# Four instead of three seven-product pairs in four of eleven gate and up groups of a two-layer decoder trunk

## The chip, the cores and the metric

The kernel runs on one core of a Trainium2 chip. The metric is the device time of one execution in microseconds (us). A core has a matrix engine (TensorE, PE in the profile), a vector engine (VectorE, DVE), a scalar engine (ScalarE, ACT), a general one (GpSimd, POOL) and a queue engine that issues most transfers (SP). Matmuls write into a separate memory (PSUM), which this kernel divides into two pools (`pa`, `pm`) of four tiles of 128 x 512 floats, called banks here; everything else lies in the core's main on-chip memory.

## The reference

Two decoder layers over 256 positions with 2048 features, in fp32. Each layer is a mixer (layer 0: sliding-window attention beside an mLSTM memory; layer 1: forgetting attention) and a SwiGLU feed-forward part (FFN), each behind an RMS norm and added to the residual stream h. The change touches the FFN:

```
def swiglu(xn, w_gate, w_up, w_down):
    return (jax.nn.silu(xn @ w_gate) * (xn @ w_up)) @ w_down
...
        h = h + swiglu(rms_norm(h, norm_ffn[layer]), w_gate[layer], w_up[layer], w_down[layer])
```

The hidden width is 5632, which is 11 blocks of 512.

## The kernel before

**Precision by three matmuls.** Each fp32 operand is split into a rounded high part (a cast on ScalarE, `hi`, `xh`, `mh`, `ht`) and a rest (a subtraction on VectorE, `lo`, `xl`, `ml`, `lt`). A product is then high by high, high by low and low by high: three matmuls into one bank (`three`). Weights come from memory as raw tiles of two k blocks (2 x 128 rows by 512 columns) and are split on the way.

**Seven products instead of eight.** `pair_group` computes two outputs at once, for example a gate block and an up block of 512 columns, each for two halves of the positions (t = 0, 1). For a *pair* of k blocks that is a 2 x 2 by 2 x 2 block product: eight block products, 24 matmuls. A *mixed* pair takes seven, 21 matmuls, after a scheme of the Strassen kind (Winograd's form): four sums of the weight blocks are formed on VectorE for each mixed pair (lines 568 to 571; `t`, `raw`) and split into `ht` and `lt`; four sums of the activations are formed once per layer by `sums_of` and kept in `sx`. Four of the seven products go into four banks of their own (`prods`), three straight into the result's banks (`plain`); at the group's end `combine` (lines 523 to 530) adds the `prods` into a tile `c` in four ways, then `c` and `plain` are added. A group therefore holds all eight banks: four from the pool `pa`, four from `pm`, changing roles from group to group.

**Order.** `ORDER` lists for a group of eight pairs which are mixed (1) and which plain (0): pairs 1, 3 and 5 are mixed, at the second, fourth and sixth place. The 11 gate and up groups of a layer (0 to 10) are taken in parts, `PARTS = (0, 3, 7, 11)`; after each part follow the two halves of the down product over the part's rows, also in `pair_group`, with two mixed pairs of six in the first part and three of eight in the others. The silu of the gate times the up result (`c`) is turned by DMA transposes of 16-bit planes, joined by copies on ScalarE (lines 646 and 653), split into `mh` and `ml`, and read by the down product; the last group of the first part is turned on TensorE. In the last down half of layer 0, `split_scaled` transposes h on TensorE for the next layer.

The order of the instructions on each engine isn't written out: a scheduler in the framework places every instruction by its own estimate of when its inputs are ready, and each engine then follows that order. The buffers that limit how far the splits run ahead are six `hi` and six `lo` tiles, two `ht`, two `lt`, and four raw tiles for mixed pairs.

Names and lines that the prediction uses: `hi` cast L177 and `lo` L178 (`split_chunk`), the same for other tiles L339 and L340 (`split_plain`), the weight sums L568 to L571, the combine L525 to L529, sums of `c` and `plain` L619, silu L621 and product L623, byte-plane copies L646 and L653, h and c L708, h and `plain` L353, transposes of h L275, the three matmuls of a product L509 to L511.

Of the kernel before, what the change touches and what calls it, by code (L numbers as in the profile page):

```python
# [17 lines left out]
P = 128  # L18
# [17 lines left out]
ORDER = ((0, 0), (1, 1), (0, 2), (1, 3), (0, 4), (1, 5), (0, 6), (0, 7))  # L36
DOWN = {
# [35 lines left out]
def trunk(  # L73
# [179 lines left out]
    def sums_of(pool, sh, sl, copies, full=None, tags=("tmp", "tmp"), bufs=None, box=None):  # L253
# [12 lines left out]
        split_plain(sh, sl, s)  # L266

    def split_scaled(idx, n, extra=None, joined=None):
        for half in range(2):
# [13 lines left out]
            if extra is not None and pair in mixed_of(ORDER):  # L283
                sh, sl, pool = extra
                j = mixed_of(ORDER).index(pair)

                def copies(full):
                    for i in range(2):
                        g = gT[:, idx * KT + 2 * pair + i : idx * KT + 2 * pair + i + 1]
                        nc.scalar.mul(full[:, i, :], pt[:, i, :, :].rearrange("p t q -> p (t q)"), g)  # L290

                sums_of(pool, sh[:, j, :, :], sl[:, j, :, :], copies)
# [200 lines left out]
    def out_proj(w, idx, key, extra):  # L493
        last, rest = KT - 4, []
        for n0 in (0, 2):
# [3 lines left out]
            for i in range(2):  # L499
# [3 lines left out]
                    (LATER[n0 + i], split_turned(idx, n0 + i, *scrap(extra[2], n0 + i), extra))  # L503
                )
                square_sum(key, n0 + i)
        return rest

# [8 lines left out]
    def pair_group(fp, par, lhs, sums, mats, order, todo=(), halves=None, inner=None, raws=None):  # L516
        plain = [[bank(par, "acc") for _ in range(NT)] for _ in range(2)]
        todo = list(todo)
# [4 lines left out]
        def combine(prods):  # L523
            c = fp.tile([P, 4, NB], F32, tag="c", name="c", bufs=1)
            nc.scalar.copy(c[:, 0, :], prods[0])  # L525
            nc.vector.tensor_tensor(out=c[:, 2, :], in0=prods[3], in1=c[:, 0, :], op=ALU.add)
# [5 lines left out]
        for pos, (kind, pair) in enumerate(order):  # L532
# [4 lines left out]
            if not kind:  # L537
# [4 lines left out]
                for m, (w, c0) in enumerate(mats):  # L542
                    hi, lo = load_chunk(w, k0, c0, NB)
                    run_due(todo, pos)
                    for i, t in walk:
# [4 lines left out]
                            pos == 0 and i == 0, last and i == CK - 1,  # L550
# [38 lines left out]
            three(plain[0][0], xb[:, t0], lb[:, t0], hg[:, 1, :], lg[:, 1, :], False, False)  # L589
            three(plain[1][0], sh[:, 3, :], sl[:, 3, :], hu[:, 1, :], lu[:, 1, :], False, False)  # L590
            three(prods[1], sh[:, 0, :], sl[:, 0, :], ht[0], lt[0], first, last)
            three(prods[2], sh[:, 2, :], sl[:, 2, :], ht[1], lt[1], first, last)
            three(prods[3], sh[:, 1, :], sl[:, 1, :], ht[2], lt[2], first, last)
            three(plain[0][1], xb[:, t1], lb[:, t1], ht[3], lt[3], False, False)
# [4 lines left out]
    def ffn(layer, fp, sx, sd, key, todo, idx_next=None, key_next=None, finish=None):  # L599
        r = rstd(key)  # L600

        def sums_x(pair):
            j = mixed_of(ORDER).index(pair)
            return sx[0][:, j, :, :], sx[1][:, j, :, :]

        for g0, g1 in zip(PARTS, PARTS[1:]):
# [3 lines left out]
            for g in range(g0, g1):  # L610
                par = (g1 - 1 - g) % 2
                plain, c = pair_group(
                    fp, par, x_of, sums_x, [(w_gate[layer], g * NB), (w_up[layer], g * NB)], ORDER, todo
                )
                todo = []
                for m in range(2):
                    for t in range(NT):
                        o = c[:, 2 * m + t, :]
                        nc.vector.tensor_tensor(out=o, in0=plain[m][t], in1=o, op=ALU.add)  # L619
                for t in range(NT):  # L620
                    nc.scalar.activation(c[:, t, :], c[:, t, :], AF.Silu, scale=r[:, t : t + 1])  # L621
                for t in range(NT):
                    nc.vector.scalar_tensor_tensor(  # L623
                        out=c[:, t, :], in0=c[:, 2 + t, :], scalar=r[:, t : t + 1], in1=c[:, t, :], op0=ALU.mult, op1=ALU.mult
# [47 lines left out]
            def sums_d(pair, order=order):  # L672
                j = mixed_of(order).index(pair)
                return sd[0][:, j, :, :], sd[1][:, j, :, :]
# [16 lines left out]
            for n0 in (0, 2):  # L691
# [20 lines left out]
    def close_layer(layer, w_out, idx, key, **rest):  # L712
        with tc.tile_pool(name=f"fp{layer}", bufs=2) as fp:
# [3 lines left out]
            todo = out_proj(w_out, idx, key, (*sx, fp))  # L717
            sd = [fp.tile([P, nd, 4, P], F32R, tag=f"sd{i}", name=f"sd{i}", bufs=1) for i in range(2)]
            ffn(layer, fp, sx, sd, key, todo, **rest)
# [22 lines left out]
    with tc.tile_pool(name="ev", bufs=1) as ev:  # L742
# [223 lines left out]
        with tc.tile_pool(name="mp", bufs=1) as mp:  # L966
            def sums_m(pair):
                j = mixed_of(MIXQ).index(pair)
                return sx[0][:, j, :, :], sx[1][:, j, :, :]
# [129 lines left out]
    with tc.tile_pool(name="od", bufs=1) as od:  # L1099
# [65 lines left out]
        def sums_x(pair):  # L1165
            j = mixed_of(MIX).index(pair)
            return sx[0][:, j, :, :], sx[1][:, j, :, :]
# [154 lines left out]
```

## Time and profile before

| | |
|---|---|
| median of 3 runs | 2077.48 us (2077.07 to 2077.85) |
| span of the profiled execution, first to last instruction | 2076.6 us |
| its own time | not given apart from the span |
| mean granted TensorE clock | 0.999 of full speed |
| memory traffic | 198 GB/s over the span |

The page lists busy time by engine, a row of tenths for 40 slices of the span, the chain of work that ended last, and the costliest groups of instructions with the idle time ahead of them and what ended it. Views of the trace cut the same records by window, line or tile; a timeline row gives the start in us, the duration, the engine, the line, output and input, and in brackets the idle time before it and who ended that. Matmuls overlap in the pipeline: a row of 0.39 us can start 0.23 us after the one before, so the distance of starts counts. A row of VectorE or ScalarE may overlap the next by some 0.08 us in the same way. Waits are put down to the last releaser.

### The profile page before, as it was taken

Reading aid. Unit: us, or ns where it says so; the run is one execution under the profiler, and the core shown is the slowest. Engines: PE = TensorE matmul, PEld = TensorE weight load, DVE = VectorE, ACT = ScalarE, POOL = GpSimd, SP = SyncE. Lnnn points to the kernel's source line nnn. Section 1 sums busy time; section 2 is a strip of 40 time slices with the busy share of each in tenths; the row PEclk is TensorE's granted clock in tenths of the full one; section 3 lists DMA queues with packets and bytes.
Section 4 is the critical chain, followed back from the end, with each engine's and each line's share of the span. In section 5 each row is a group of like instructions: output and inputs, shape, how many; then the busy total and the mean of one; then the engine's idle time right before and its main releaser. Section 6 shows DMA issues by size and latency. Waiting matters only on the chain.

```text
span 2076.6 us, 26994 instructions
## 1 busy us (share of the span) xinstructions
PE 2066.4 (100%) x9473; PEld 1715.0 (83%) x9473; DVE 1824.5 (88%) x2410; ACT 1374.7 (66%) x1736; POOL 41.7 (2%) x66
## 2 busy tenths in 40 slices
PE   9999999999999999999999999999999999999998
PEld 7878888888888888888888888888888888888887
DVE  6788769999999999999899778689999999999994
ACT  6777678765676656667676776687655667456763
POOL 1010000000000000000000001000000000000000
PEclk9999999999999999999999999999999999999999
DMA  8566577666566666666576866586665667666764
GB/s 292 172 213 188 190 247 236 203 217 206 189 230 223 205 210 205 220 212 204 185 215 204 235 193 184 156 283 220 206 205 200 213 206 234 203 202 213 220 197 138
DMA packets 309575, 434.87 MB, mean 209 GB/s; under 512 B 106412, under 2 KB 114624, under 8 KB 309312
## 3 DMA queue, kind: packets, MB, share of 16 engines
q1 hardware_dynamic: 307088, 426.27, 65.1%
q0 software_dynamic: 1632, 5.80, 0.8%
q8 instruction: 74, 1.21, 0.2%
q10 hardware_dynamic: 720, 1.09, 0.2%
q14 instruction: 61, 0.50, 0.1%
HBM read 408.68 MB, written 2.12 MB: 198 GB/s over the span
## 4 chain that ended last, share of the span: by engine, by line
PE 97%; DVE 1%; ACT 1%; DMA 1%; issue 1%; SPq 0%; POOLq 0%; POOL 0%; ACTq 0%; DVEq 0%
PE acc L510 21%; PE acc L509 21%; PE acc L511 21%; PE acc L213 5%; PE acc L212 5%; PE acc L214 5%; PE prod L509 5%; PE prod L510 5%; PE prod L511 5%; PE p L369 1%; PE po L470 1%; DMA raw<-in_w_in_odd_dram 0%; ACT s L403 0%; PE po L471 0%; DVE lo L178 0%
## 5 line engine op out<-in xcount | busy, mean ns | idle before, releaser
L177 ACT CAST hi<-raw 128x1024 fp32r<-128x1024 f32 (+3 forms) x656 | 664.8, 1028 | 440.2 <-PE acc L511 269.1
L178 DVE TENSOR_TENSOR lo<-raw,hi 128x1024 fp32r<-128x1024 f32 (+3 forms) x656 | 772.8, 1192 | 146.3 <-ACT hi L177 143.5
L510 PE MATMUL acc<-lo,xh 128*128 128x512 f32 x1254 | 488.6, 390 | 0.0
L509 PE MATMUL acc<-hi,xh 128*128 128x512 f32 x1254 | 485.9, 390 | 0.5 <-ACT hi L177 0.5
L511 PE MATMUL acc<-hi,xl 128*128 128x512 f32 x1254 | 484.8, 389 | 0.0
L510 PEld LDWEIGHTS acc<-lo,xh 128*128 128x128 f32 x1254 | 235.4, 188 | 49.4 <-DVE lo L178 0.6
L509 PEld LDWEIGHTS acc<-hi,xh 128*128 128x128 f32 x1254 | 235.2, 188 | 49.5 <-ACT hi L177 0.7
L511 PEld LDWEIGHTS acc<-hi,xl 128*128 128x128 f32 x1254 | 235.4, 188 | 48.8
L510 PE MATMUL acc<-lo,mh 128*128 128x512 f32 x437 | 169.7, 389 | 0.0
L511 PE MATMUL acc<-hi,ml 128*128 128x512 f32 x437 | 168.4, 389 | 0.0
L509 PE MATMUL acc<-hi,mh 128*128 128x512 f32 x437 | 167.9, 389 | 0.0
L339 ACT CAST hi<-raw 128x512 fp32r<-128x512 f32 x109 | 67.6, 620 | 89.4 <-PE acc L511 80.5
L213 PE MATMUL acc<-lo,mh 128*128 128x512 f32 (+1 forms) x322 | 126.3, 392 | 0.0
L212 PE MATMUL acc<-hi,mh 128*128 128x512 f32 (+1 forms) x322 | 125.8, 391 | 0.0
L214 PE MATMUL acc<-hi,ml 128*128 128x512 f32 (+1 forms) x322 | 123.7, 391 | 0.0
L340 DVE TENSOR_TENSOR lt<-t,ht 128x1024 fp32r<-128x1024 f32 x95 | 115.8, 1219 | 5.2 <-ACT ht L339 5.1
L339 ACT CAST ht<-t 128x1024 fp32r<-128x1024 f32 x95 | 99.9, 1051 | 30.7 <-PE prod L511 28.8
L339 ACT CAST ht<-raw 128x1024 fp32r<-128x1024 f32 x95 | 99.7, 1050 | 29.7 <-PE acc L511 15.0
L340 DVE TENSOR_TENSOR lt<-raw,ht 128x1024 fp32r<-128x1024 f32 x95 | 115.7, 1218 | 1.8 <-ACT ht L339 1.8
L213 PE MATMUL acc<-lo,xh 128*128 128x512 f32 (+3 forms) x288 | 99.8, 348 | 0.2 <-DVE lo L178 0.2
L214 PE MATMUL acc<-hi,xl 128*128 128x512 f32 (+3 forms) x288 | 98.1, 344 | 0.0
L212 PE MATMUL acc<-hi,xh 128*128 128x512 f32 (+3 forms) x288 | 95.9, 347 | 0.3
(363 smaller groups left out, 3448.0 us busy)
## 6 DMA issues: line engine op xcount, KB each, us to landing
raw<-in_w_gate_dram SPq DMA_DIRECT2D x176, 512.0 KB, 4.5
raw<-in_w_up_dram SPq DMA_DIRECT2D x176, 512.0 KB, 4.6
raw<-in_w_down_dram SPq DMA_DIRECT2D x176, 512.0 KB, 5.1
raw<-in_w_in_odd_dram SPq DMA_DIRECT2D x88, 512.0 KB, 4.9
raw<-in_w_in_even_dram SPq DMA_DIRECT2D x51, 512.0 KB, 5.0
raw<-in_w_out_even_dram SPq DMA_DIRECT2D x32, 512.0 KB, 5.1
raw<-in_w_out_odd_dram SPq DMA_DIRECT2D x32, 512.0 KB, 4.8
hr<-in_w_in_even_dram SPq DMA_DIRECT2D x12, 512.0 KB, 4.6
```

The source lines that it names most:

```text
L177: latest[0] = nc.scalar.copy(hi[:, k, 0:n], raw[:, k, 0:n])
L178: nc.vector.tensor_tensor(out=lo[:, k, 0:n], in0=raw[:, k, 0:n], in1=hi[:, k, 0:n].bitcast(F32), op=ALU.subtract)
L212: nc.tensor.matmul(o, ah[:, ts], hi, start=(k == 0), stop=False)
L213: nc.tensor.matmul(o, ah[:, ts], lo, start=False, stop=False)
L214: nc.tensor.matmul(o, al[:, ts], hi, start=False, stop=(k == k_all - 1 and cs.stop == n))
L339: nc.scalar.copy(dst_h, src)
L340: nc.vector.tensor_tensor(out=dst_l, in0=src, in1=dst_h.bitcast(F32), op=ALU.subtract)
L369: nc.tensor.matmul(pq[j % 2][:, j // 2, :], q_of(j, b), k_of(j)[:, 0:cols], start=True, stop=True)
L470: nc.tensor.matmul(po, v_of(j, 0), tt[:, j, 0:2, :].rearrange("p c q -> p (c q)"), start=True, stop=False)
L509: nc.tensor.matmul(o, ah, hi, start=start, stop=False)
L510: nc.tensor.matmul(o, ah, lo, start=False, stop=False)
L511: nc.tensor.matmul(o, al, hi, start=False, stop=stop)
```

## The change

In groups 1, 4, 6 and 8 of each layer (`DENSE`) a fourth pair, number 7, is mixed as well. The order of these groups (`HEAVY`) begins with a mixed pair and alternates. The activation sums of pair 7 are made when the others are (in `split_scaled`); three of the four sums are stored in those blocks of `xh` and `xl` that no product of the FFN reads, the t = 1 halves of the first k block of the mixed pairs 1, 3 and 5 (`rooms`), the fourth in a small tile `x4`. To make room for it the descriptor space of POOL's transfers is halved. Whether a matmul is the first into a bank (`start`) is now found by a record (`fresh`).

Where `halves` isn't used, that is in all FFN groups, `combine` has another layout of `c` (t before m) and other association: two sums of 512 columns and one of 1024 in place of four of 512. The sums of h and `c` in the down halves become two of 1024 instead of four of 512. `four` hands the sums over as lists; `sums_d` and the mixers' `sums_m` and `sums_x` use it with no change of meaning.

```
+HEAVY = ((1, 1), (0, 0), (1, 3), (0, 2), (1, 5), (0, 4), (1, 7), (0, 6))
+FOURTH = 7
+DENSE = (1, 4, 6, 8)
...
-    def sums_of(pool, sh, sl, copies, full=None, tags=("tmp", "tmp"), bufs=None, box=None):
+    def sums_of(pool, sh, sl, copies, full=None, tags=("tmp", "tmp"), bufs=None, box=None, x4=None):
...
-        split_plain(sh, sl, s)
+        if x4 is None:
+            split_plain(sh, sl, s)
+        else:
+            split_plain(sh, sl, s[:, 0:3, :])
+            split_plain(x4[:, 0, :], x4[:, 1, :], s[:, 3, :])
...
-            if extra is not None and pair in mixed_of(ORDER):
-                sh, sl, pool = extra
-                j = mixed_of(ORDER).index(pair)
+            if extra is not None and (pair in mixed_of(ORDER) or pair == FOURTH):
+                sh, sl, x4, pool = extra
...
+                if pair == FOURTH:
+                    sums_of(pool, rooms(xh), rooms(xl), copies, x4=x4)
+                else:
+                    j = mixed_of(ORDER).index(pair)
+                    sums_of(pool, sh[:, j, :, :], sl[:, j, :, :], copies)
...
+    def four(s, j):
+        return [s[:, j, e, :] for e in range(4)]
+
+    def rooms(m):
+        return m[:, 2:11:4, P:S]
...
+            if halves is None:
+                nc.vector.tensor_tensor(out=c[:, 1, :], in0=prods[3], in1=c[:, 0, :], op=ALU.add)
+                nc.vector.tensor_tensor(out=c[:, 2, :], in0=prods[2], in1=c[:, 1, :], op=ALU.add)
+                nc.vector.tensor_tensor(
+                    out=c[:, 1:4:2, :],
+                    in0=prods[1].rearrange("p (a n) -> p a n", a=1).broadcast_to([P, 2, NB]),
+                    in1=c[:, 1:3, :],
+                    op=ALU.add,
+                )
+                return c
...
         def sums_x(pair):
+            if pair == FOURTH:
+                return [[m[:, k, P:S] for k in (2, 6, 10)] + [x4[:, a, :]] for a, m in enumerate((xh, xl))]
...
-                    fp, par, x_of, sums_x, [(w_gate[layer], g * NB), (w_up[layer], g * NB)], ORDER, todo
+                    fp,
+                    par,
+                    x_of,
+                    sums_x,
+                    [(w_gate[layer], g * NB), (w_up[layer], g * NB)],
+                    HEAVY if g in DENSE else ORDER,
+                    todo,
...
-                for m in range(2):
-                    for t in range(NT):
-                        o = h[:, t, (n0 + m) * NB : (n0 + m + 1) * NB]
-                        nc.vector.tensor_tensor(out=o, in0=c[:, 2 * m + t, :], in1=o, op=ALU.add)
+                for t in range(NT):
+                    o = h[:, t, n0 * NB : (n0 + 2) * NB]
+                    nc.vector.tensor_tensor(
+                        out=o, in0=c[:, 2 * t : 2 * t + 2, :].rearrange("p a n -> p (a n)"), in1=o, op=ALU.add
+                    )
...
+            x4 = fp.tile([P, 2, P], F32R, name="x4", bufs=1)
...
-    nc = _bacc.Bacc("TRN2", target_bir_lowering=False, num_devices=1, dynamic_dma_scratch_size=4096)
+    nc = _bacc.Bacc("TRN2", target_bir_lowering=False, num_devices=1, dynamic_dma_scratch_size=2048)
```

More of the change, by code (lines that the diff above doesn't have):

```diff
@@ L517, in pair_group, with fresh @@
         plain = [[bank(par, "acc") for _ in range(NT)] for _ in range(2)]
+        begun = set()
+        def fresh(*at):
+            known = at in begun
+            begun.add(at)
+            return not known
         todo = list(todo)
@@ L549, in pair_group @@
                             plain[m][t], ah[:, ts], al[:, ts], hi[:, i, :], lo[:, i, :],
-                            pos == 0 and i == 0, last and i == CK - 1,
+                            fresh(m, t), last and i == CK - 1,
                         )
```

40 lines of the change are left out of this document (22 added, 18 removed).

## The prediction

> **What bounds the kernel now.** I read the page first: busy time by engine, then the chain that ended last.
>
> ```profile
> PE 2066.4 (100%) x9473; PEld 1715.0 (83%) x9473; DVE 1824.5 (88%) x2410; ACT 1374.7 (66%) x1736; POOL 41.7 (2%) x66
> ...
> PE 97%; DVE 1%; ACT 1%; DMA 1%; issue 1%; SPq 0%; POOLq 0%; POOL 0%; ACTq 0%; DVEq 0%
> ```
>
> TensorE is busy all the time and carries 97% of the chain; VectorE, at 88%, is next. An average hides the stage, so I cut the first layer's FFN at the ScalarE copies that begin each combine (the timeline of ScalarE), one window per group: groups 4 to 5, 5 to 6, 6 to the down product, and its two halves.
>
> ```profile
> 662.30 0.58 ACT L525 COPY c<-prod 128x512 f32<-128x512 f32 x1
> ...
> 703.78 0.58 ACT L525 COPY c<-prod 128x512 f32<-128x512 f32 x1
> ```
> ```profile
> core 0: us, PE busy (x) PEld busy (x) DVE busy (x) ACT busy (x) POOL busy (x), PEclk, DMA share, GB/s
> 579.34:620.82 41.48, 41.48 (x185) 34.35 (x184) 39.72 (x51) 28.52 (x32) 0.00 (x0) 1.00 0.66 214
> 620.82:662.30 41.48, 41.48 (x185) 34.35 (x184) 39.73 (x51) 28.47 (x33) 0.00 (x0) 1.00 0.66 216
> 662.30:703.78 41.48, 41.48 (x185) 34.35 (x184) 39.93 (x48) 28.07 (x32) 0.00 (x0) 1.00 0.68 216
> 703.78:745.26 41.48, 41.48 (x185) 34.35 (x184) 39.32 (x47) 21.90 (x24) 0.00 (x0) 1.00 0.65 207
> 745.26:786.74 41.48, 41.48 (x185) 34.35 (x184) 38.52 (x46) 21.86 (x25) 0.00 (x0) 1.00 0.67 214
> ```
>
> A group takes 41.48 us, five times running. It has 5 pairs of 24 matmuls and 3 of 21, so 183 (the counts of 185 include some that straddle a cut): 41.48 / 183 = 0.2267 us each. TensorE never waits here, and VectorE is busy for 39.7 of 41.48 us: only 1.8 us of slack in a gate-and-up group, 2.2 and 3.0 in the down halves. So the stage has one limit and a second one 4% behind it. How far VectorE runs ahead is seen by setting its last part of a pair against the matmul that reads it first (timelines of VectorE and TensorE):
>
> ```profile
> 649.56 1.23 DVE L178 TENSOR_TENSOR lo<-raw,hi 128x1024 fp32r<-128x1024 f32 x1 [1.08 <-ACT hi L177]
> 650.70 0.69 DVE L568 TENSOR_TENSOR t<-raw 128x512 f32<-128x512 f32 x1
> 651.30 0.68 DVE L569 TENSOR_TENSOR t<-raw 128x512 f32<-128x512 f32 x1
> 651.90 1.22 DVE L340 TENSOR_TENSOR lt<-raw,ht 128x1024 fp32r<-128x1024 f32 x1
> 653.04 0.69 DVE L570 TENSOR_TENSOR raw<-raw,t 128x512 f32<-128x512 f32 x1
> ...
> 658.36 1.22 DVE L340 TENSOR_TENSOR lt<-t,ht 128x1024 fp32r<-128x1024 f32 x1
> ```
> ```profile
> 663.64 0.39 PE L510 MATMUL prod<-lt,sx 128*128 128x512 f32 x1
> ```
>
> The lt written at 658.36 ends at 659.58 and is read at 663.64: a lead of 4.06 us, among the shortest of the group. That is the reserve.
>
> **The change, part by part.** *Removed on TensorE*: in a dense group a pair of 24 matmuls becomes one of 21; 4 groups, 2 layers: 24 matmuls x 0.2267 = **5.44 us**, all on the path. That is 0.26%, just above the 0.2% (4.2 us) that a measurement of this kernel can tell from no change.
>
> *Added on VectorE*, per dense group: start to start, a pass over 1024 columns takes 1.14 us (649.56 to 650.70) and one over 512 takes 0.60 (650.70 to 651.30). A plain pair costs two lo passes, 2.28. A seven-product pair costs one lo, two lt (3 x 1.14) and four differences and the half lo (5 x 0.60): 6.42. So +4.14 us. The combine replaces two 512 passes by one of 1024: -0.06; each down half does the same twice for h: -0.12. The fourth pair's sums, once per layer inside group 0, are four passes of 128 columns and two short splits:
>
> ```profile
> 656.11 0.29 DVE L262 TENSOR_TENSOR s<-c 128x128 f32<-128x128 f32 x1
> 656.32 0.28 DVE L264 TENSOR_TENSOR s<-c 128x128 f32<-128x128 f32 x1
> ```
>
> 4 x 0.21, and for the splits between 0.21 and 0.60 each: 1.7 us at most, ahead of the first dense group.
>
> A dense group is thus 39.72 + 4.08 = 43.8 us of VectorE against 183 - 3 = 180 matmuls, 40.80 us: 3.0 over. Groups 4 to 6 (dense, not, dense) sum to 43.8 + 39.7 + 44.0 = 127.5 against 40.8 + 41.5 + 40.8 = 123.1 us: 4.4 over, with a reserve of 4.06. On average it fits (the down halves give 2.2 + 3.0 back), but the reserve is gone where group 6 ends.
>
> *Moved*: the scheduler orders every engine anew, and the built program shows that it no longer finds cover everywhere. In the trace of before each engine's instructions stand in the built order, so a chain can be added up by hand: from a matmul that frees a buffer to the matmul that needs its successor. Durations for that, from ScalarE's groups between 600 and 800 us, and the step from a last read to the next cast:
>
> ```profile
> L177 ACT CAST hi<-raw 128x1024 fp32r<-128x1024 f32 x63 | 65.1, 1052 | 52.1 <-PE acc L511 44.0 <-issue 3.8 <-ACT ht L339 2.9
> ...
> L339 ACT CAST ht<-raw 128x1024 fp32r<-128x1024 f32 x15 | 15.8, 1050 | 7.0 <-PE acc L511 5.6 <-DVE raw L571 1.4
> ...
> L653 ACT COPY c<-turned 128x1024 uint16<-128x1024 uint16 x6 | 7.9, 1357 | 0.0
> ```
> ```profile
> 673.84 0.39 PE L511 MATMUL acc<-hi,xl 128*128 128x512 f32 x1
> ```
> ```profile
> 674.26 1.06 ACT L177 CAST hi<-raw 128x1024 fp32r<-128x1024 f32 x1 [2.10 <-PE acc L511]
> ```
>
> The cast starts 0.42 us after the start of the matmul that freed its buffer; a cast takes 1.05 (0.96 when another follows), a copy of a turned tile 1.27.
>
> 1. *Group 1 to 2, both layers.* In ScalarE's queue a hi cast that waits for a last read stands directly ahead of the ht cast of the dense group's last pair, which TensorE needs three matmuls after that read. 0.42 + 0.96 + 1.05 = 2.43 against 0.68: a wait of **1.75**. Bounds: 0.5 if the ht cast comes first after all, 3.1 if VectorE's backlog of that group is paid here as well.
> 2. *Group 2 to the down halves, both layers.* Here the activations are turned on TensorE itself, and VectorE's queue from the combine to the last split is longer than its matmuls by 1.2 (bounds 0.3 and 3.0): **1.2**.
> 3. *Group 6 to its down half, both layers.* First, a hi buffer is read for the last time one matmul before its successor is needed: 0.42 + 1.05 - 0.23 = 1.25. Then the down half's seventh pair needs the transposed activations; ahead of their cast ScalarE has two hi casts, two copies, and an ht cast: 0.42 + 3 x 0.96 + 2 x 1.27 + 1.05 = 6.9 against 21 matmuls, 4.76: 2.1. These short steps alone are 3.4. The long chain, from the ht cast after group 5's combine to the same activations: ScalarE's head 2.9; on VectorE 19 passes of 1024 (21.6), 23 of 512 (13.9), small ones 2.2; ScalarE's tail (two byte-plane copies, then the queue above with one more hi cast) 9.3. Together 49.8 us, against 193 matmuls, 43.75: **6.0**, the short steps within it.
>
> In the trace of before the same activations have ample time:
>
> ```profile
> 697.47 1.22 DVE L340 TENSOR_TENSOR ml<-c,mh 128x1024 fp32r<-128x1024 f32 x1
> ```
> ```profile
> 707.84 0.39 PE L511 MATMUL acc<-hi,ml 128*128 128x512 f32 x1
> ```
>
> 9.2 us from their end to their first read; in the built order of after nothing of it is left.
>
> 4. *End of layer 0.* The last products of the down half end 15 matmuls (3.4 us) before the transposes of h. In before it is thus:
>
> ```profile
> 1004.57 0.39 PE L511 MATMUL prod<-ht,sd 128*128 128x512 f32 x1
> ```
> ```profile
> 1005.00 0.69 DVE L526 TENSOR_TENSOR c<-prod,c 128x512 f32<-128x512 f32 x1 [2.26 <-PE prod L511]
> 1005.73 0.69 DVE L527 TENSOR_TENSOR c<-prod,c 128x512 f32<-128x512 f32 x1
> ```
> ```profile
> 1012.80 0.27 PE L275 MATMUL pt<-ident,h 128*128 128x128 f32 x1
> ```
>
> 8.2 us lie between, filled with the next projection's matmuls. In after, the transposes wait for: 0.42, two sums (1.2), the wide sum (1.14), two wide h sums (2.28, each over both column blocks, so the first needs more than before), two short lo passes (1.3) and one h sum (0.69): 7.0 against 3.4, a wait of **3.6** (bounds 2.2 and 3.8).
>
> **Sum.** 2 x (1.75 + 1.2 + 6.0) + 3.6 = 21.5 us of new waits, less 5.44: +16.1. The profiled execution spans 2076.6 us, 0.9 below the median of the three runs, 2077.48; its own time is not given apart, so the sum is put on the median: **2093.5 us**. By the low ends, 2 x (0.5 + 0.3 + 3.4) + 2.2 = 10.6, less 5.44: 2082.6. By the high ends, 2 x (3.1 + 3.0 + 6.2) + 3.8 = 28.4: 2100.4. POOL's descriptor space is halved; I cost that at nothing, because the loads that use it are few and early (DMA issues, and VectorE's timeline for the first reader of h): h is asked for by POOL at 222 to 224 us, lands in 7.5 and is first needed at 276.
>
> ```profile
> h<-in_x_dram POOLq DMA_DIRECT2D x4, 512.0 KB, 7.5
> ```
> ```profile
> L1092 POOL DMA_DIRECT2D h<-in_x_dram x4: 722/723/730, 222.1 to 224.2; - x4
> ```
> ```profile
> 276.19 1.29 DVE L353 TENSOR_TENSOR h<-acc,h 128x512 f32<-128x512 f32 x2 [2.45 <-PE acc L214]
> ```
>
> **Rivals.** *A, VectorE keeps up: faster.* The reserve of 4.06 us absorbs the 4.4, and the short ScalarE steps are covered, so that all waits together stay below 1.3 us. Place: groups 4 to 6; price: the removed matmuls alone, 2072.0 to 2073.3. For it: no wait of TensorE in this stage now, and the average slack. Against: the queue orders above, which hold whatever the backlog.
>
> *B, the waits are there but small:* 1.3 to 9.6 us of them, 2073.3 to 2081.6, no change that can be told. A third of each term above, 2 x 3.0 + 1.2 = 7.2, gives 2079.2. For it: the chains are added from single rows, and a stretch of 50 us that is 4% shorter than counted takes 2 us off step 3. Against: the short steps, which hold few rows, make 2 x (1.75 + 3.4) + 3.6 = 13.9 by themselves.
>
> *C, the waits feed on themselves:* the clock falls. If after each of the three longest waits the next 15 matmuls took twice 0.2267, that is 3 x 3.4 = 10.2 us more: 2103.7. The clock column is 1.00 in every window above; no wait of that length is in them, so the trace can't show it. [...]
>
> **Chances.** Forecast (2082 to 2101) 0.69; A 0.09; B 0.15; C or more 0.07. From these: faster by over 0.2% 0.09, within 0.2% 0.15, slower 0.76. The range leaves out A, the lower half of B and the upper part of C: 2077 to 2102.
>
> **What would show it.** In the profile of after: 24 fewer matmuls of 512 columns; four-difference passes 8 more per line; waits of TensorE for ScalarE's ht and hi casts where group 1 ends, for the activations' cast some 24 us into the down half after group 6, for h at the transposes at the end of layer 0; the windows of dense groups at 40.80 where nothing waits; the same places in layer 1. Wrong if TensorE has no idle time in these windows (then A), if group 8 waits as much as group 6, or if the clock column leaves 1.00 (then C). If short waits stand where named but the long chain's 6 us doesn't, the size of step 3 is off.

## The result and the profile after

| | before | after |
|---|---|---|
| median of the runs, us | 2077.28 (2076.80 to 2077.85, 4 runs) | 2113.57 (2111.82 to 2115.21, 4 runs) |
| span of the profiled execution, us | 2076.6 | 2110.1 |
| mean granted clock | 0.999 | 0.997 |

The changed kernel is slower: ratio 1.0174, 95% interval 1.0159 to 1.0188, or 36.3 us. The direction was forecast; the time lies 20 us above the forecast of 2093.5 and above its range. The profiled execution is the fastest of the four (2111.82 us), 34.5 us above the kernel before.

The page of the changed kernel, busy time and chain:

```profile
PE 2073.6 (98%) x9449; PEld 1710.7 (81%) x9449; DVE 1854.7 (88%) x2415; ACT 1387.9 (66%) x1760; POOL 43.2 (2%) x66
...
PE 85%; DVE 7%; DMA 3%; issue 2%; ACT 2%; SPq 0%; POOLq 0%; POOL 0%; DVEq 0%; ACTq 0%
```

The 24 matmuls are gone (9473 to 9449), and yet the chain has lost 12 points of TensorE to VectorE, transfers and ScalarE. Whom TensorE waited for (view of its waits: sum in us, times, longest):

```profile
PE prod L526 <- DVE lt L350: 5.1, 5, 1.6
PE acc L525 <- ACT mh L349: 5.0, 4, 1.6
PE prod L525 <- ACT ht L349: 4.4, 4, 2.5
PE pt L282 <- DVE h L363: 3.7, 1, 3.7
PE acc L525 <- ACT hi L180: 2.3, 2, 1.1
PE acc L525 <- ACT c L548: 1.9, 2, 1.1
PE acc L525 <- ACT hi L349: 1.5, 2, 0.8
```

In the FFN none of these waits was there before. Windows of 20 us over layer 0 (columns as in the windows of before; the number behind PE's busy time counts its matmuls):

```profile
400.00:420.00 20.00, 17.55 (x69) 13.54 (x68) 18.69 (x25) 10.14 (x13) 0.00 (x0) 0.91 0.58 184
...
440.00:460.00 20.00, 17.68 (x74) 13.37 (x73) 16.99 (x24) 12.17 (x14) 0.00 (x0) 1.00 0.77 240
460.00:480.00 20.00, 19.05 (x88) 15.53 (x87) 19.57 (x24) 12.81 (x16) 0.00 (x0) 1.00 0.69 224
660.00:680.00 20.00, 17.71 (x76) 13.49 (x74) 14.57 (x21) 15.84 (x18) 0.00 (x0) 1.00 0.53 152
680.00:700.00 20.00, 17.90 (x74) 13.54 (x75) 20.00 (x24) 8.81 (x10) 0.00 (x0) 1.00 0.72 237
700.00:720.00 20.00, 19.49 (x85) 15.51 (x83) 20.00 (x24) 16.65 (x17) 0.00 (x0) 1.00 0.67 171
720.00:740.00 20.00, 18.73 (x81) 15.20 (x82) 18.33 (x21) 10.62 (x12) 0.00 (x0) 1.00 0.76 258
```

A full window holds 90 matmuls (those that straddle an edge included), so a missing one stands for 20 / 90 = 0.222 us. The first three windows (groups 1 and 2 and the first down halves) lack 21 + 16 + 2 = 39, 8.7 us; the other four (the end of group 6 and the down halves behind it) lack 14 + 16 + 5 + 9 = 44, 9.8 us. Counted in the same way, windows below 89 only, layer 1 lost 5.6 and 9.3 us. All other FFN windows are full, those around group 8 among them. This count is the measure of the experiments below: it takes in waits, the gaps at their edges and a slower clock alike.

TensorE at the wait of 2.45 us (timeline):

```profile
404.13 0.50 PE L525 MATMUL prod<-ht,xh 128*128 128x512 f32 x1 [2.45 <-ACT ht L349]
...
406.23 0.63 PE L525 MATMUL acc<-hi,xh 128*128 128x512 f32 x1
406.66 0.63 PE L526 MATMUL acc<-lo,xh 128*128 128x512 f32 x1
```

Behind the wait the matmuls start 0.43 us apart (406.23 to 406.66), not 0.227. Of the 4.7 us that this window lost, the wait is 2.45; the clock, 0.91 of 20 us, is 1.8.

ScalarE ahead of the waits of 660 to 700 us, and TensorE at the end of layer 0:

```profile
661.95 1.05 ACT L349 CAST ht<-raw 128x1024 fp32r<-128x1024 f32 x1
662.90 1.99 ACT L692 COPY c<-c 128x1024 uint16<-128x1024 uint16 x2
667.86 1.35 ACT L699 COPY c<-turned 128x1024 uint16<-128x1024 uint16 x1 [2.96 <-DMA turned<-c]
669.16 1.05 ACT L349 CAST ht<-t 128x1024 fp32r<-128x1024 f32 x1
670.42 1.36 ACT L699 COPY c<-turned 128x1024 uint16<-128x1024 uint16 x1 [0.20 <-DMA turned<-c]
671.64 1.04 ACT L349 CAST ht<-raw 128x1024 fp32r<-128x1024 f32 x1
```
```profile
1029.71 0.69 PE L282 MATMUL pt<-ident,h 128*128 128x128 f32 x2 [3.73 <-DVE h L363]
```

The byte planes of group 5 are copied out (L692) and, as the next thing on ScalarE, copied back (L699): it stands still for 2.96 us until the turning transfers have landed, with the ht casts of dense group 6 queued behind. They end near 670 and 673. The lt for which TensorE waits at 676 is made later still, at 674.98, because of a load. SyncE's queue, VectorE and TensorE at this place:

```profile
663.97 5.12 SPq L694 DMA_TRANSPOSE turned<-c  x4
669.19 0.53 SPq L126 DMA_DIRECT2D raw<-in_w_up_dram  x1
```
```profile
673.57 0.69 DVE L601 TENSOR_TENSOR t<-raw 128x512 f32<-128x512 f32 x1 [1.27 <-DMA raw<-in_w_up_dram]
```
```profile
676.26 0.50 PE L526 MATMUL prod<-lt,sx 128*128 128x512 f32 x1 [1.56 <-DVE lt L350]
```

The four turning transfers occupy SyncE's queue for 5.12 us, and the load of the up tile of pair 7, the fourth mixed pair of group 6, stands behind them. It is asked for at 669.19, and VectorE, which has the first weight difference of pair 7 (L601) ahead of the lt of the pair before, waits for it until 673.57. The hi cast of the same tile is the one for which TensorE waits at 674. In layer 1 the same rows stand at 1738.91, 1744.13, 1748.61 (1.36) and 1751.30 (1.58).

### The profile page after: what moved, and what is told of

The parts are those of the page before. It is cut to its first block, busy times and chain, and to the rows that moved or that the text cites. A ratio compares the mean times of both kernels' runs of the same rounds, so it can differ in the third digit from the quotient of the medians.

```text
span 2110.1 us, 26965 instructions
## 1 busy us (share of the span) xinstructions
PE 2073.6 (98%) x9449; PEld 1710.7 (81%) x9449; DVE 1854.7 (88%) x2415; ACT 1387.9 (66%) x1760; POOL 43.2 (2%) x66
## 4 chain that ended last, share of the span: by engine, by line
PE 85%; DVE 7%; DMA 3%; issue 2%; ACT 2%; SPq 0%; POOLq 0%; POOL 0%; DVEq 0%; ACTq 0%
PE acc L525 18%; PE acc L526 17%; PE acc L527 17%; PE acc L216 5%; PE acc L215 5%; PE acc L217 5%; PE prod L525 5%; PE prod L527 4%; PE prod L526 4%; DVE lo L181 2%; DMA raw<-in_w_down_dram 2%; DVE lt L350 1%; DMA raw<-in_w_up_dram 1%; PE p L379 1%; PE po L480 1%
## 5 line engine op out<-in xcount | busy, mean ns | idle before, releaser
L181 DVE TENSOR_TENSOR lo<-raw,hi 128x1024 fp32r<-128x1024 f32 (+3 forms) x648 | 761.8, 1190 | 115.7 <-ACT hi L180 112.5
L526 PE MATMUL acc<-lo,xh 128*128 128x512 f32 x1198 | 467.2, 390 | 0.0
L527 PE MATMUL acc<-hi,xl 128*128 128x512 f32 x1198 | 463.8, 390 | 0.0
L525 PE MATMUL acc<-hi,xh 128*128 128x512 f32 x1198 | 461.2, 391 | 0.1
L525 PEld LDWEIGHTS acc<-hi,xh 128*128 128x128 f32 x1198 | 225.1, 188 | 48.3 <-DVE c L551 0.8
L526 PEld LDWEIGHTS acc<-lo,xh 128*128 128x128 f32 x1198 | 225.2, 188 | 47.3 <-DVE lo L181 0.8
L527 PEld LDWEIGHTS acc<-hi,xl 128*128 128x128 f32 x1198 | 225.2, 188 | 47.0
L350 DVE TENSOR_TENSOR lt<-t,ht 128x1024 fp32r<-128x1024 f32 x103 | 125.6, 1219 | 23.5 <-ACT ht L349 22.7
L350 DVE TENSOR_TENSOR lt<-raw,ht 128x1024 fp32r<-128x1024 f32 x103 | 125.3, 1217 | 3.2 <-ACT ht L349 3.0
L349 ACT CAST ht<-raw 128x1024 fp32r<-128x1024 f32 x103 | 108.0, 1049 | 13.7 <-PE acc L527 10.2
L525 PEld LDWEIGHTS acc<-hi,mh 128*128 128x128 f32 x437 | 82.0, 188 | 31.6 <-ACT mh L349 6.4
```

Source lines behind the costliest of these rows:

```text
L181: nc.vector.tensor_tensor(out=lo[:, k, 0:n], in0=raw[:, k, 0:n], in1=hi[:, k, 0:n].bitcast(F32), op=ALU.subtract)
L349: nc.scalar.copy(dst_h, src)
L350: nc.vector.tensor_tensor(out=dst_l, in0=src, in1=dst_h.bitcast(F32), op=ALU.subtract)
L525: nc.tensor.matmul(o, ah, hi, start=start, stop=False)
L526: nc.tensor.matmul(o, ah, lo, start=False, stop=False)
L527: nc.tensor.matmul(o, al, hi, start=False, stop=stop)
```

## The experiments

All kernels are edits of the changed one. The table counts lost time as above, and gives the median and the matmuls left out (x 0.2267 us); the sections say what was asked. Beside these kernels the kernel before took 2077.2 to 2077.9.

| kernel | median, us | matmuls saved, us | groups 1, 2 and down: layer 0, 1 | groups 3 to 10 and down: layer 0, 1 |
|---|---|---|---|---|
| changed | 2113.57 | 5.4 | 8.7, 5.6 | 9.8, 9.3 |
| no dense group | 2081.10 | 0 | 0, 0 | 0, 0 |
| new order alone | 2087.55 | 0 | 4.9, 2.7 | 0, 0 |
| new order, old combine and sums | 2079.49 | 0 | 0, 0.9 | 0, 0 |
| dense, weight sums left out | 2088.57 | 5.4 | 5.1, 3.6 | 0, 0 |
| VectorE's load alone in 4, 6 | 2097.40 | 0 | 0, 0 | 8.2, 8.4 |
| dense 1 | 2095.54 | 1.4 | 8.0, 7.8 | 0, 0 |
| dense 6 | 2084.88 | 1.4 | 0, 0 | 2.7, 2.4 |
| dense 4, 6 | 2098.60 | 2.7 | 0, 0 | 10.2, 10.7 |
| dense 8 | 2082.47 | 1.4 | 0, 0 | 0, 0 |
| dense 3, 7, old combine and sums | 2084.02 | 2.7 | 0, 0 | 4.2, 3.3 |
| differences on GpSimd | 2124.90 | 5.4 | 11.6, 8.7 | 11.8, 15.3 |
| all dense, old combine and sums | 2102.37 | 5.4 | 3.1, 5.8 | 9.6, 7.6 |
| all dense, old sums of h | 2103.23 | 5.4 | 8.9, 6.4 | 4.7, 5.1 |

Where the end of layer 0 stays as it is without dense groups, the columns account for the times: dense 4 and 6 is 2081.1 - 2.7 + 20.9 = 2099.3, measured 2098.6; dense 1 is 2081.1 - 1.4 + 15.8 = 2095.5, measured 2095.5.

### What the parts around the dense groups cost

No dense group; then the sums of h undone as well; then combine and layout too.

```
-DENSE = (1, 4, 6, 8)
+DENSE = ()
```
```
+                for m in range(2):
+                    for t in range(NT):
+                        o = h[:, t, (n0 + m) * NB : (n0 + m + 1) * NB]
+                        nc.vector.tensor_tensor(out=o, in0=c[:, 2 * t + m, :], in1=o, op=ALU.add)
```

> No group takes a fourth mixed pair; all else of the change stays (the other combine and layout of c, the merged sums of h, the fourth pair's activation sums, the halved descriptor space). Load theory (VectorE and ScalarE get 4 us more work per dense group than the lead allows): the waits of the FFN groups go; what may stay is the 3.7 us wait for h at the end of layer 0 with its clock dip, so 2077 to 2083 us. Rival 'surroundings' (layout, sums of h, descriptor space): most of the loss stays, 2100 us or more.

> No dense groups, and the sums of h and c in the down halves are four of 512 columns again, all else as changed. Without dense groups TensorE waited 1.70 us for h at the end of layer 0, where before it waited for nothing of note. Theory 'merged sums' (the first of the two sums covers what the transposes don't need yet, so h comes a pass of 512 columns late): that wait goes, 2079 to 2080 us. Rival 'combine' (the other order of the combine ends it later): it stays, 2081 us.

> No dense groups, and combine, layout of c and sums of h are those of before; what stays of the change is the fourth pair's activation sums, their place, the record of first matmuls and the halved descriptor space. Theory 'combine and merged sums': the time of before within 1 us, 2077 to 2078.5. Rival 'activation sums and descriptor space': 2080 to 2082 us.

Measured: 2081.10 (ratio 1.0017, 1.0008 to 1.0027), 2079.26 (1.0008, 0.9998 to 1.0017) and 2077.49 (0.9997, 0.9988 to 1.0007). No FFN wait above 0.6 us is left in the first; it waits 1.70 us for h at the end of layer 0, and without the merged sums that wait is gone. So merged sums and new combine cost 1.8 us each by the medians (the kernel before took 2077.24 beside the first and 2077.69 beside the other two), although they save VectorE time; the fourth pair's activation sums, their place and the halved descriptor space cost nothing that shows.

### The order, or VectorE's load

Pair 7 plain in the new order; the same with the old combine, layout and sums of h; then the dense groups with VectorE's weight sums of pair 7 left out, so that its products take the plain tiles; then VectorE's load in groups 4 and 6 without any dense group.

```
-HEAVY = (..., (1, 5), (0, 4), (1, 7), (0, 6))
+HEAVY = (..., (1, 5), (0, 4), (0, 7), (0, 6))
```
```
+            if kind and pair == FOURTH and ...:
+                (hg, lg), (hu, lu) = (load_chunk(w, k0, c0, NB) for w, c0 in mats)
...
+                three(prods[1], sh[0], sl[0], hu[:, 0, :], lu[:, 0, :], False, True)
+                three(prods[2], sh[2], sl[2], hu[:, 1, :], lu[:, 1, :], False, True)
...
```
```
-                    HEAVY if g in DENSE else ORDER,
+                    ORDER,
...
+                    if extra and pair == FOURTH:
+                        t4 = fp.tile([P, 2, NB], F32, tag="t4", name="t4", bufs=1)
+                        a, b = hi.bitcast(F32), lo.bitcast(F32)
+                        if m == 0:
+                            nc.vector.tensor_tensor(out=t4, in0=a, in1=b, op=ALU.add)
+                        for n in range(2 + m):
+                            nc.vector.tensor_tensor(out=t4[:, n % 2, :], in0=a[:, n % 2, :], in1=b[:, n % 2, :], op=ALU.add)
```

> The dense groups keep the order that begins with a mixed pair, but pair 7 is plain at its place, so no product is saved and VectorE has the work of before. Load theory: within 2 us of the kernel without dense groups, 2077 to 2085 us. Rival 'order' (a mixed pair at the first place asks for the four banks of the products and for ht and lt too early): its waits stay, 15 to 30 us, 2095 to 2110 us.

> The order that begins with a mixed pair in groups 1, 4, 6 and 8, pair 7 plain, with combine, layout and sums of h of before. With the new ones this order alone took 2087.6 us, 6.5 more than the old order, through waits at the turned group 2 in both layers (4.9 and 2.7 us of matmuls missing). Theory 'the order alone moves a cast that waits for a weight transfer ahead of the mh cast': the waits stay, 2083 to 2086 us (6.5 over 2077.5). Rival 'it takes the new combine too': 2077 to 2079 us.

> The dense groups stay as they are, with 21 matmuls for pair 7, but the four weight sums of pair 7 are left out: its products take the plain hi and lo tiles, so VectorE has 2.28 us for this pair as before and TensorE has 24 matmuls less. Load theory: nearly all FFN waits go and the saving shows, 5.4 us less than without dense groups: 2071 to 2079 us. Rivals 'order' and 'surroundings': waits stay, 2095 to 2113 us.

> No group takes a fourth mixed pair and the order is the old one everywhere; but in groups 4 and 6 VectorE gets, at pair 7, the passes that a fourth mixed pair would have added: one of 1024 and five of 512 columns, 4.14 us by the trace of before, with results that nothing reads. TensorE's and ScalarE's work is that of the kernel without dense groups (2081.1 us), so TensorE has 41.48 and not 40.80 us for these groups. Load theory: VectorE needs 43.9 in each, 2.4 over and over again, the lead is spent in group 6: 2 to 8 us lost per layer, 2085 to 2097 us. Rival 'chain' (what costs is the longer way through ScalarE's ht casts and the two ht and lt buffers, not VectorE's time): 2080 to 2083 us.

Measured: 2087.55, 2079.49, 2088.57, 2097.40. The load theory holds for groups 4 to 6: with 21 matmuls but without the sums these windows are full, and with the load alone, the old order and no product saved, TensorE loses 8.2 and 8.4 us there, at the top end of the forecast. Some 6.8 of these 16.6 us are the clock, granted 0.83 in one window of layer 0, 0.88 and 0.95 in two of layer 1; TensorE waits four times for an ht cast, 8.0 us in all, at most 2.4 at once. Windows of the kernel without the sums, then of the one with the load alone:

```profile
680.00:700.00 20.00, 20.00 (x90) 16.57 (x89) 19.35 (x25) 14.42 (x16) 0.00 (x0) 1.00 0.65 181
700.00:720.00 20.00, 20.00 (x90) 16.57 (x89) 19.57 (x20) 12.61 (x14) 0.00 (x0) 1.00 0.78 262
```
```profile
680.00:700.00 20.00, 19.84 (x88) 16.11 (x87) 20.00 (x25) 12.06 (x13) 0.00 (x0) 1.00 0.46 139
700.00:720.00 20.00, 15.21 (x55) 11.22 (x54) 17.11 (x20) 14.45 (x16) 0.00 (x0) 0.83 0.84 259
```

It fails for groups 1 and 2: 5.1 and 3.6 us stay without the sums, 4.9 and 2.7 with the order alone, and so the theory missed the first and the third time (the third also by a wait of 3.74 us for h at the end of layer 0); the rivals' 2095 us and more weren't reached either. ScalarE in the kernel with the order alone, then in the kernel before:

```profile
466.94 1.05 ACT L180 CAST hi<-raw 128x1024 fp32r<-128x1024 f32 x1 [4.18 <-DMA raw<-in_w_down_dram]
467.89 1.07 ACT L349 CAST mh<-pf 128x512 fp32r<-128x512 f32 x2
```
```profile
459.58 1.05 ACT L177 CAST hi<-raw 128x1024 fp32r<-128x1024 f32 x1 [4.13 <-PE prod L511]
```

The cast of the turned activations (mh), for which TensorE waits, stands behind a cast of weights that land at 466.9; in the trace of before the cast ahead of mh was released by a matmul. With the old combine and sums the wait for mh is gone; waits of 0.98 and 1.30 us for the combine's copy (L548) stand in its place, 0.9 us by the count and 2.0 by the medians (2079.49 against 2077.49), near the rival's forecast. So the wait for mh comes from where the scheduler puts one cast, and not from VectorE's load.

### Which groups

`DENSE` holds one or two groups; the last with combine, layout and sums of h as before.

```
-DENSE = (1, 4, 6, 8)
+DENSE = (1,)          # then (6,), (4, 6), (8,), and (3, 7)
```

> Only group 1 of each layer is dense (1.36 us of matmuls fewer). Without any dense group the kernel takes 2081.1 us. Load theory: the waits at the end of group 1 (about 4.8 and 2.9 us in the changed kernel) and those of the turned group 2 (5 and 3) both come from group 1: 2081.1 - 1.4 + 15 = 2095 us, 2090 to 2098. Rival 'together' (the loss needs the four dense groups together): 2080 to 2084 us.

> Only group 6 of each layer is dense; 6 matmuls fewer, 1.36 us. Load theory: group 6 needs 44.0 us of VectorE against 40.8 of TensorE, 3.2 over with a lead of 4.06, and group 4 has not spent the lead before it, so the wait at the down half shrinks from about 10 us per layer to 0 to 3: 2076 to 2085 us. Rival 'place' (a dense group right ahead of the down product costs by itself): the loss of about 20 us for both layers stays, 2093 to 2100 us.

> Groups 4 and 6 are dense (2.7 us of matmuls fewer). Load theory: what group 4 takes from the lead is not given back by group 5, which has 1.8 us of slack on VectorE, so group 6 starts behind: 9.5 us lost in each layer as in the changed kernel, 2081.1 - 2.7 + 19 = 2097 us, 2093 to 2100. Rival 'no memory' (each dense group costs by itself; group 6 alone lost 2.7 per layer): 2081.1 - 2.7 + 5.4 = 2084, up to 2087 us.

> Only group 8 is dense. Load theory: groups 9 and 10 and the lead ahead of them cover 3.0 us, so nothing but the 1.36 us saved and perhaps the longer wait for h at the end of layer 0 (2 us): 2079.7 to 2082. Rival 'place' (every dense group costs 5 us or more in each layer): 2088 us or more.

> Groups 3 and 7 are dense, the first groups behind a down product; combine, layout and sums of h are those of before. 12 matmuls fewer, 2.7 us. Load theory: the down halves ahead leave VectorE 2.2 and 3.0 us, and the groups behind have 1.8 us of slack each before the next down product, so the 3.0 us over are covered and nothing is lost: 2.7 us under the same kernel without dense groups, 2074 to 2077 us. Rival 'every place costs' (the order that begins with a mixed pair, or the handing over of banks behind a down half): 2082 to 2090 us.

Measured: 2095.54, 2084.88, 2098.60, 2082.47 and 2084.02. Groups 4 and 6 together lose 20.9 us, group 6 alone 5.1, and group 4's own windows are full in all of these kernels: what a group takes from the lead is paid by the next dense one. Some 7 of the 20.9 us are the clock, granted 0.91, 0.91, 0.92 and 0.91 in four windows of 20 us (from 660, 700, 1720 and 1780 us). Group 8 loses nothing in its windows; but at the end of layer 0 TensorE then waits 3.74 us for h, not 1.70, and it ends 1.4 us above the kernel without dense groups, 0.5 above the forecast. The theory was wrong for 3 and 7, the first groups behind a down half: 7.5 us lost, 6.0 of them where group 7 ends (800 and 1860 us), so the slack of the down halves is no lead that the next group finds.

### Relief by GpSimd

```
+            eng = nc.gpsimd if pair == FOURTH and halves is None and order is HEAVY else nc.vector
-            nc.vector.tensor_tensor(out=ta, in0=rb[:, 0, :], in1=ra[:, 0, :], op=ALU.subtract)
+            eng.tensor_tensor(out=ta, in0=rb[:, 0, :], in1=ra[:, 0, :], op=ALU.subtract)
...
```

> The changed kernel, but the four weight differences of pair 7 in the dense groups are made on GpSimd, which is busy for 2% of the span, in place of VectorE. VectorE's surplus in a dense group shrinks from 4.14 to 1.74 us (5 x 0.60 less 4 x 0.60 stay), so a dense group needs 41.4 against 40.8 us. Load theory: nearly all that groups 4 and 6 lost (9.5 per layer) is won back, and part of group 1's: 2113.6 - 19 - 0 to 12 = 2083 to 2095 us. Rival 'chain' (the way from the weights through the differences, ht and lt to the matmul is too long, and GpSimd, whose time for such a pass no trace of this case shows, makes it longer): 2108 us or more.

Measured: 2124.90 us (ratio 1.0227, 1.0212 to 1.0242), 11 us worse than the changed kernel. GpSimd and VectorE in the same stretch:

```profile
394.39 2.22 POOL L602 TENSOR_TENSOR t<-raw 128x512 f32<-128x512 f32 x1 [62.51 <-DVE lt L350]
396.57 2.28 POOL L603 TENSOR_TENSOR t<-raw 128x512 f32<-128x512 f32 x1
398.81 1.34 POOL L604 TENSOR_TENSOR raw<-raw,t 128x512 f32<-128x512 f32 x1
```
```profile
394.23 1.22 DVE L181 TENSOR_TENSOR lo<-raw,hi 128x1024 fp32r<-128x1024 f32 x1
395.36 2.33 DVE L350 TENSOR_TENSOR lt<-raw,ht 128x1024 fp32r<-128x1024 f32 x1
397.61 1.38 DVE L265 TENSOR_TENSOR s<-c 128x128 f32<-128x128 f32 x1
398.91 1.38 DVE L267 TENSOR_TENSOR s<-c 128x128 f32<-128x128 f32 x1
400.22 0.28 DVE L266 TENSOR_TENSOR s<-s,c 128x128 f32<-128x128 f32 x1
```

GpSimd takes 1.3 to 2.3 us, roughly timed, for a pass that VectorE does in 0.69, and VectorE's passes of the meantime take 2.33 in place of 1.22 and 1.38 in place of 0.28. So VectorE wins nothing, and the way to ht and lt is longer. The rival's forecast holds; that VectorE's own passes take 1.1 us longer, neither theory had. The row at 400.22, behind GpSimd's last pass (to 400.15), takes 0.28 again; why the others are longer wasn't shown.

### Do the parts act on each other

All four dense groups, with the old combine, layout and sums of h; then with the old sums of h alone.

> The changed kernel with its four dense groups, but combine, layout and sums of h of before. Without dense groups these parts cost 3.6 us (2081.1 against 2077.5). Theory 'the costs add': 2113.6 - 3.6 = 2110 us, 2107 to 2112. Rival 'the new combine shortens the chains at the group ends' (two sums fewer wait for the four products' banks): 2114 us or more.

> The changed kernel with its dense groups and its combine, but with the four sums of 512 columns for h in the down halves. Theory 'the combine reacts with the dense groups': merged sums are worth only the 1.8 us that they were without dense groups, so 2110 to 2112.5 us; the other 9 us of the 11.2 between the changed kernel and the one with both old parts belong to the combine. Rival 'the merged sums are the larger part': 2102 to 2106 us.

Measured: 2102.37 and 2103.23 us. The first misses both of its forecasts, the second meets the rival's (2102 to 2106): merged sums of h cost 10.3 us beside the dense groups and the new combine, and 1.8 without. VectorE's work is nearly the same in both; the loss of groups 3 to 10 falls from 9.8 and 9.3 to 4.7 and 5.1 where the built order is another. ScalarE and SyncE's queue with the old sums of h, at the place shown above for the changed kernel:

```profile
661.96 2.00 ACT L692 COPY c<-c 128x1024 uint16<-128x1024 uint16 x2 [0.89 <-DVE c L664]
665.89 0.62 ACT L349 CAST hi<-raw 128x512 fp32r<-128x512 f32 x1 [1.94 <-DMA raw<-in_w_up_dram]
...
667.37 1.05 ACT L349 CAST ht<-t 128x1024 fp32r<-128x1024 f32 x1
...
669.27 1.37 ACT L699 COPY c<-turned 128x1024 uint16<-128x1024 uint16 x1
```
```profile
661.23 0.37 SPq L126 DMA_DIRECT2D raw<-in_w_up_dram  x1
663.03 5.14 SPq L694 DMA_TRANSPOSE turned<-c  x4
```

The same planes are copied out at the same time, but the joining copy stands four casts later and waits for nothing, and the up tile of pair 7 is asked for ahead of the turning transfers, not behind them. Over the whole trace ScalarE waited for these transfers 21.7 us in the changed kernel and 8.7 here (rows of the two views of ScalarE's waits):

```profile
ACT c L699 <- DMA turned<-c: 21.7, 15, 3.0
```
```profile
ACT c L699 <- DMA turned<-c: 8.7, 10, 1.5
```

In the kernel before, ScalarE never waited for them. But merged sums as such don't bring this order about: with the old combine and the old sums of h the copy waits 2.97 us again (at 661.3), the up tile is asked for behind the turning transfers (at 662.67), ScalarE waits 17.1 us for them in all, and 9.6 and 7.6 us are lost. What that kernel gains on the changed one lies in groups 1 and 2 (8.9 lost and not 14.3) and in the parts around. So each of these edits changes the order that the scheduler builds; why it builds this one wasn't traced, and no run moves that one load by itself.

With all four groups dense the lost windows leave 4 to 5 us unexplained (here with the old combine: 2077.5 - 5.4 + 26.1 = 2098.2 against 2102.4). Most of it lies at the end of layer 0: 2.9 us in the changed kernel, and in the other two waits for h of 1.94 and 1.86 us. Behind the second the matmuls of 272 columns start 0.23 us apart up to 1029.3, then 0.125: the clock is at half for some 3.5 us. The same kernels without dense groups have no such wait, and a mean granted clock of 0.999 where these two have 0.997.

### The clock

Group 8 alone dense, and three matmuls that nothing reads put where TensorE waits for h.

```
+                if cover and n == 2 and half == 0:
+                    for _ in range(3):
+                        nc.tensor.matmul(
+                            pt.rearrange("p i t q -> p (i t q)"), ident, cover[-1][:, 3, :], start=True, stop=True
+                        )
```

> Only group 8 dense as in the earlier run (2082.5 us), and three matmuls of 128x512 with results that nothing reads stand on TensorE where it waited 3.74 us for h at the end of layer 0; the granted clock there was 0.50 for 6.8 us behind that wait. Theory 'clock' (the wait itself costs 3.7 us and the halved clock behind it another 3.4): the wait for h ends no earlier, but the clock stays at 1.00 and 3 us come back: 2079 to 2080 us. Rival 'wait alone' (the clock's record costs nothing, TensorE waits on VectorE there anyway): 2082 to 2083 us.

Measured: 2081.59 us; span 2079.5 against 2081.2. TensorE and windows without, then with the fillers:

```profile
1013.06 0.47 PE L282 MATMUL pt<-ident,h 128*128 128x128 f32 x1 [3.74 <-DVE h L363]
```
```profile
1012.00:1018.00 6.00, 4.94 (x22) 4.94 (x23) 4.71 (x12) 2.89 (x8) 0.69 (x1) 0.50 0.87 254
```
```profile
1012.96 0.44 PE L289 MATMUL pt<-ident,h 128*128 128x128 f32 x2 [1.16 <-DVE h L370]
```
```profile
1012.00:1018.00 6.00, 5.04 (x42) 5.04 (x43) 4.99 (x13) 3.78 (x11) 0.69 (x1) 1.00 0.83 242
```

h comes at the same time, but the clock stays at 1.00 and TensorE does 42 matmuls, not 22, in the 6 us behind it. The clock theory holds; its price was too high, 1.7 us by the spans (0.9 by the medians) and not 3.

### Is there a place that pays

Groups 4 and 8 in both layers, and group 4 in both with 8 in layer 1 alone; combine, layout and sums of h as before.

> Groups 4 and 8 are dense, each the second of its part; combine, layout and sums of h are those of before. 12 matmuls fewer, 2.7 us, from the 2077.5 us of the same kernel without dense groups. Theory 'second place is free' (neither group 4 nor group 8 showed a wait of its own; but group 8 came with a wait of 3.7 us for h and a halved clock at the end of layer 0, about 3.4 us): 2076 to 2079 us. Rival 'the end of layer 0 was the merged sums' doing': 2074.8 us. Rival 'every place costs' (groups 3 and 7 lost 9.3 us): 2080 to 2085 us.

> Group 4 of both layers and group 8 of layer 1 are dense, combine, layout and sums of h as before: 9 matmuls fewer, 2.0 us from 2077.5 us. Theory 'second place is free' and the end of layer 0 is untouched: 2075.4 us, below the kernel before. Rival 'every place costs': 2079 to 2083 us.

Measured: 2079.86 us (ratio 1.0010, 1.0002 to 1.0019) and 2078.66 (1.0004, 0.9995 to 1.0013), both above what 'second place is free' had forecast and below 'every place costs'. The first waits 1.96 us for h at the end of layer 0. The second is level with the kernel before: it saves 2.0 us and loses 1.6 at 700 us, where TensorE waits 0.9 us for an ht cast behind group 6. No version was faster than before, and with 5.4 us at stake in all, none could be by much.

## Why the prediction was right or wrong

**The bound, and the sign.** Right. VectorE is the second limit 4% behind TensorE, and the 4.14 us per dense group are what costs in groups 4 and 6: alone, with no product saved, they lose 16.6 us over the two layers, 6.8 of it by the clock. That "the reserve is gone where group 6 ends" is what the pair 4, 6 shows against 6 alone.

**Removed.** Right: 24 matmuls.

**Steps 1 and 2** (1.75 + 1.2 = 2.95 per layer, upper bounds 6.1): place right, size wrong, 8.7 and 5.6 measured. TensorE did wait for the ht cast where group 1 ends, 2.45 and 1.63 us. In layer 1 the cast ahead is released by a matmul's last read, as the step has it; in layer 0 ScalarE stood still 1.34 us for the landing of an up tile (until 401.57), two casts ahead of that ht. What the working lacked is this transfer, the clock behind the longer wait (1.8 us), and at group 2 the cast that waits for a weight transfer ahead of mh; the chain there counted VectorE's queue alone.

**Step 3** (6.0 per layer, bounds 3.4 and 6.2): mis-sized, 9.8 and 9.3. Its short steps came near: TensorE waits 1.13 us for the hi cast at 694.9 (forecast 1.25) and 1.60 for the activations' cast at 721.3 (2.1). The long chain took the way through the turned activations at busy durations, and two things aren't in it: ScalarE's wait for the turning transfers (2.96 us), and SyncE's queue, in which the load of pair 7's up tile stands behind them. So the first waits come at 674 and 676, in the last pairs of group 6, ahead of the down half where the step expected them. With the old sums of h, where neither is so, 4.7 and 5.1 are lost, less than the 6.0.

**Step 4** (3.6): right, 3.73, of which 1.70 are there without dense groups; the halved clock behind it (0.50 from 1029.7 to 1033) comes on top.

**The edits costed at less than nothing.** This price failed outright. "The combine replaces two 512 passes by one of 1024: -0.06; each down half does the same twice for h: -0.12" priced these edits by VectorE's time. The combine and the merged sums cost 3.6 us by themselves, and 11.2 beside the dense groups (2113.57 against 2102.37): besides the 3.6, 5.4 in groups 1 and 2 and 1.9 in groups 3 to 10. The built orders differ there; which part of them costs how much is shown by single rows only. Without these edits the kernel would have taken 2102.4, at the upper end of the range.

**The terms together.** Steps 1 and 2 measured 14.3 where 5.9 was summed, step 3 19.1 where 12.0 was, and these two make up 15.5 of the 20 us. Their chains run from a matmul that frees a buffer to the matmul that needs its successor and hold neither the transfer between them nor its place in SyncE's queue, and no halved clock.

**Rival C.** The forecast's sum holds no halved clock, and there it was wrong: behind the waits of 2.45 and 3.73 us the clock fell to half (0.50 from 405 to 408 and from 1029.7 to 1033). That 15 matmuls then take twice their time was C's assumption, which no trace of before showed; at 405 eight matmuls in a row took 0.41 to 0.43 us from start to start. C's price, three times 3.4, was too high: 1.8 us at 405, and at the end of layer 0 about 0.9, half of what the fillers won back, for the clock was halved there for some 3.5 us (1029.6 to 1033.1) and for 6.9 (1011.7 to 1018.6) in the kernel with group 8 alone.

**Group 8** waits for nothing, as forecast; that **A** and **B** fail is shown by the windows. **Descriptor space** at nothing: right (2077.49 with it).

The sum by the runs: 3.8 for the parts around, 33.4 lost in the windows, some 2.9 at the end of layer 0 (3.73 against 1.70, and 0.9 of clock), less 5.4: 34.7 us. The profiled execution, from which the windows come, was 34.5 us above the kernel before; the median is 36.3 above.

## What to carry to other kernels

Here VectorE was 4% behind TensorE (39.7 of 41.48 us in a group) with a lead of some 4 us, and work moved to it was paid once the lead was spent: 5.1 us lost with group 6 alone dense, 20.9 with 4 and 6. An average didn't give the lead back: ask for each group how much slack lies between it and the next one. Under a scheduler, an edit of two vector instructions must be judged by the order that it causes on every in-order queue, above all by casts that come to stand behind a wait for a transfer and by loads behind other transfers in the issuing queue; its own duration says little. A run with the suspected load alone and one with every edit but that load tell these two apart.

## What was not expected of the hardware

- Half clock followed waits of TensorE of 2.45 us (changed kernel, 0.50 from 405 to 408) and 1.86 us (all groups dense, old sums of h, to 1029.3), and 1.77 us without a matmul between 712 and 715 (all groups dense, old combine and sums, 0.50 from 716 to 719). Behind a wait of 1.60 us in the changed kernel (at 721) it stayed at 1.00, as it did behind 1.71 us with the old sums of h (at 716) and 1.96 us with groups 4 and 8 dense (end of layer 0). So the length of the wait alone doesn't decide.
- Three rows of VectorE that began while GpSimd worked took 1.1 us longer: 2.33 in place of 1.22 us for 1024 columns, 1.38 in place of 0.28 for 128 (twice).
